# Another order of the seven products of a Strassen-Winograd feed-forward layer, and of the output blocks behind them

## The chip, the core and the metric

One Trainium2 chip, one core of it. The metric is the device time of the whole program in microseconds (us), lower is better. Below, PE is TensorE, DVE is VectorE, ACT is ScalarE, and SP issues the DMAs. "mm" is short for matmul.

## What is computed

A decoder trunk of two layers on 512 positions of width 1024, in float32: layer 0 mixes with a gated MLP and latent attention, layer 1 with gated linear attention. Both end in the same feed-forward half, and the change touches that half alone:

```python
def sqrelu_mlp(x, w1, w2):
    return jnp.square(jax.nn.relu(x @ w1)) @ w2
...
x = layer_norm(ALPHA * x + sqrelu_mlp(x, w_ff1[layer], w_ff2[layer]), ln2_g[layer], ln2_b[layer])
```

`x` is 512 x 1024, `w1` 1024 x 4096, `w2` 4096 x 1024; h = square(relu(x @ w1)) is 512 x 4096.

## The kernel before

**Precision.** Every float32 operand is split into two float32r parts, hi and lo; a product is three matmuls (hi hi, hi lo, lo hi). `split` (L163 to L165) does this for a weight: ACT casts hi (L164), then DVE subtracts lo (L165).

**First product.** `ff` (L283) cuts the 4096 columns of h into 8 groups g of 2 x 256 columns. A group is a 2 x 2 block product: rows of x in two halves, its depth in two halves, and the columns from the left and the right half of w1. Group 0 is done plainly with eight block products. Groups 1 to 7 use seven products of sums (Strassen in Winograd's form): P1, P2, and p3 to p7, listed in `PRODUCTS` (L278). Each is 24 mm of 256 columns (`mul`, L444). Sums of x (s1 to s4) are made once and kept in tiles s2h/s2l, s3h/s3l, s4h/s4l; s1 takes the place of a block of x. Product p3 reads s4, p7 reads s3, p6 reads s2. Sums of weights (t1 to t4) are made on DVE in `sum1` (L369), in place.

**From products to h.** The products go to five PSUM banks a to e (`RELEASED`, L442): P1 and P2 to a, p3 to c, p4 and p7 to d, p5 to e, p6 to b. `product` (L463) issues a product and then whatever has become possible:

```python
            step("V", {"p1s", "p6"}, lambda: nc.vector.tensor_tensor(V, bk("b"), V, ALU.subtract))
            step("X", {"V", "p5"}, lambda: nc.vector.tensor_tensor(X, V, bk("e"), ALU.subtract))
            step("C11", {"P2"}, lambda: relu2(g, 0, 0, bk("a")))
            step("C22", {"X", "p7"}, c22)
            step("C12", {"X", "p3"}, c12)
            step("C21", {"V", "C22", "p4"}, c21)
```

So block C22 of h (second half of the rows, second half of the columns) needs V (L497), X (L498) and r = X - d (L485) on DVE; C12 needs c = X - c (L489); C21 needs d = d - V (L493); C11 comes from its bank directly. Bank d holds p7 until L485 has read it, and only then may p4 be added to it. Each block then goes through `relu2` (L423): ACT relu (L428), ACT square (L429), ACT cast to hh (L430), DVE subtraction hl (L431). The last of these is put in a list `late` and issued by `flush` just before the next product or the next half.

**Second product.** `ff2_half(c, n, t)` (L504) multiplies row block t (128 rows) of h by 256 + 256 rows of w2 for 512 columns n: 12 mm of 512 columns. Blocks t = 0, 1 read C11 for their first 6 mm and C12 for the other 6; t = 2, 3 read C21 and then C22. A chunk c is eight halves, n = 0, 1 by t = 0 to 3; DVE adds each half to the residual XN (L208). Chunk 1 follows group 1 at once, chunk 2 group 2; then come groups 3 and 4 in a row, so that chunks 3, 4, 5 each use blocks that are a group old. Group 7 is followed at once by the close, in which the last two chunks are one sum: for t = 0 first, per n, 6 mm + 6 mm of chunk 6 and then 6 mm of C11 and 6 mm of C12 of group 7 (`close_mm`, L594).

**What sets the order.** PE's order is written out in `slots` (L514 to L522) and kept. DVE's order is that of the program text in this part. ACT's and SP's orders are chosen by a scheduler when the program is built. `wseq` is the order in which weights are loaded and split; `upto` (L543) runs it ahead of PE by up to 6 entries. Split weights of w1 and w2 go through 8 pairs of tiles (whi, wlo). The last four weights of a layer, those of the close for n = 1, go elsewhere (`LAST`, L384, `pair`, L376): the first of them to s4h/s4l, the second to s3h/s3l, the third to s2h/s2l, the fourth to two other tiles. In the profile these four are called ws, and so are three weights of group 0.

Of the kernel before, what the change touches and what calls it, by code (L numbers as in the profile page):

```python
# [22 lines left out]
NT = S // P  # L23
# [80 lines left out]
def trunk(ctx: ExitStack, tc: tile.TileContext, a: dict, out: bass.AP):  # L104
# [179 lines left out]
    def ff(layer, hp, fp, xp, out_proj, prefetch):  # L284

        w1, w2 = a["w_ff1"][layer], a["w_ff2"][layer]
# [68 lines left out]
        def load1(g, n):  # L355

            for m in (n,) if g == 0 else {"B11": ("B11", "B12"), "B21": ("B21",), "t1": ("B22",)}.get(n, ()):
                if g == 0 and m != "B22":
                    raw = wp.tile([P, WG], F32, tag="raw", name="raw", bufs=3)
                elif g == 0 or m in ("B11", "B12"):  # L360
                    raw = xp.tile([P, WG], F32, tag="cr", name="cr", bufs=2)
                else:
                    if g not in kept2:
                        kept2[g] = xp.tile([P, 2, WG], F32, tag="xk", name="cr2")
                    raw = kept2[g][:, m == "B21"]
                raws[g, m] = raw
                nc.sync.dma_start(raw.rearrange("p (k c) -> p k c", k=HK_), w1v(*BLOCK[m], g))

        def sum1(g, n):  # L369

            if n in SUM and (g, n) not in raws:
                x, y = SUM[n]
                raws[g, n] = raws[g, x]
                nc.vector.tensor_tensor(raws[g, n], raws[g, x], raws[g, y], ALU.add)
# [11 lines left out]
        def terms1(g, n):  # L386
            sum1(g, n)
            raw = raws[g, n]
            if (g, n) == (0, "B22"):
                his = [hp.tile([P, HK_, P], F32R, tag="hh", name="wh") for _ in range(2)]  # L390
                los = [hp.tile([P, HK_, P], F32R, tag="hl", name="wl") for _ in range(2)]
                for j in range(2):
                    split(his[j], los[j], raw.rearrange("p (k c) -> p k c", k=HK_)[:, :, tb(j)])
            else:
                hi, lo = pair(EARLY[n] if g == 0 else None)
                split(hi, lo, raw)
                his, los = ([z.rearrange("p (k c) -> p k c", k=HK_)[:, :, tb(j)] for j in range(2)] for z in (hi, lo))
            got_w[g, n] = his, los

        def load2(c, n, half):  # L400
            r = half * 2048 + c * GF
            raw = wp.tile([P, WG], F32, tag="raw", name="raw", bufs=3)
            nc.sync.dma_start(raw.rearrange("p (k c) -> p k c", k=2),
                              w2[r:r + GF, n * 512:(n + 1) * 512].rearrange("(k p) c -> p k c", p=P))
            raws["w2", c, n, half] = raw

        def terms2(c, n, half):
            raw = raws.pop(("w2", c, n, half))
            hi, lo = pair(LAST[(c - NG + 2) * 2 + half] if c >= NG - 2 and n == 1 else None)
            split(hi, lo, raw)  # L410
            v = lambda x: x.rearrange("p (k c) -> p k c", k=2)
            got_w["w2", c, n, half] = v(hi), v(lo)
# [24 lines left out]
        def flush():  # L437
            while late:
                late.pop(0)()
# [23 lines left out]
        def product(g, n):  # L463

            first = (g, RELEASED[n]) not in banks
            if first:
                banks[g, RELEASED[n]] = bank("f1")
            acc = banks[g, RELEASED[n]]
            op, w = PRODUCTS[n]
            mul(acc, op, got_w.pop((g, w)), first)  # L470
            done = state.setdefault(g, set())
            done.add(n)
            V = LG[:, g % 2 * 512:(g % 2 + 1) * 512]
            X = LB[:, g % 2 * 512:(g % 2 + 1) * 512]
            bk = lambda z: banks[g, z]
            hq.setdefault(g, {})

            def step(name, needs, fn):
                if name not in done and needs <= done:
                    done.add(name)  # L480
                    fn()

            def c22():
                r = scratch(g)
                nc.vector.tensor_tensor(r, X, bk("d"), ALU.subtract)  # L485
                relu2(g, 1, 1, r, r)

            def c12():
                nc.vector.tensor_tensor(bk("c"), X, bk("c"), ALU.subtract)  # L489
                relu2(g, 0, 1, bk("c"))  # L490

            def c21():
                nc.vector.tensor_tensor(bk("d"), bk("d"), V, ALU.subtract)  # L493
                relu2(g, 1, 0, bk("d"))

            step("p1s", {"P1"}, lambda: nc.scalar.copy(V, bk("a")))
# [7 lines that stand above are left out]
        def ff2_half(c, n, t):  # L504
            acc = bank("f2")
            i, tc_ = t // 2, slice(t % 2 * P, (t % 2 + 1) * P)
            for k in range(4):
                hh, hl = hq[c][i, k // 2]
                wh, wl = got_w["w2", c, n, k // 2]
                mm3(acc, hh[:, k % 2, tc_], hl[:, k % 2, tc_], wh[:, k % 2], wl[:, k % 2], k == 0, k == 3)  # L510
            add_half(t, n, acc, c == 0, None)


        LATER = ("P1", "p5", "p7", "p6", "p3", "P2", "p4")  # L514
        slots, wseq = [], []

        def put_group(g):
            slots.extend((g, n) for n in LATER)
            wseq.extend((g, n) for n in ("B11", "t1", "t3", "t2", "B22", "B21", "t4"))

        def put_chunk(c):
            slots.extend(("w2", c, n, t) for n in range(2) for t in range(NT))  # L522
            wseq.extend(("w2", c, n, h) for n in range(2) for h in range(2))

        wseq += [(0, n) for n in ("B11", "B21", "B12", "B22")]
        put_chunk(0)

        mid = NG // 2 - 1
        for c in range(1, NG - 2):
            for g in (c,) if c < mid else (c, c + 1) if c == mid else (c + 1,):  # L530
                put_group(g)
            put_chunk(c)
        put_group(NG - 1)
        wseq += [("w2", c, n, h) for n in range(2) for c in (NG - 2, NG - 1) for h in range(2)]
        for i, w in enumerate(wseq):
# [5 lines left out]
        LOADS, TERMS = 6, 6  # L541

        def upto(n, loads=None):  # L543

            while at["load"] < min(len(wseq), n + (LOADS if loads is None else loads)):
                w = wseq[at["load"]]
                at["load"] += 1
                (load2(*w[1:]) if w[0] == "w2" else load1(*w))
            while at["terms"] < min(len(wseq), n):
                w = wseq[at["terms"]]  # L550
                i = at["terms"]
                at["terms"] += 1
                if w[0] != "w2":
                    sum1(*w)
                if i + 1 < at["load"] and wseq[i + 1][1] in SUM and wseq[i + 1] != (w[0], "t1"):
                    sum1(*wseq[i + 1])
                (terms2(*w[1:]) if w[0] == "w2" else terms1(*w))
# [16 lines left out]
        for i, s in enumerate(slots):  # L574
            if s[0] == "w2":
                need = max(place["w2", s[1], s[2], 1], place["w2", s[1], s[2], 0])
                if s[1] == 0:
                    next(sums, None)
                    upto(max(need + 1, 8 + i // 2))
                else:  # L580
                    upto(min(need + 1 + TERMS, need + 1 + 2 * (s[3] + 1)))
                flush()
                ff2_half(s[1], s[2], s[3])
                continue
            upto(place[s[0], PRODUCTS[s[1]][1]] + 1 + min(TERMS, 2 + s[0]))
            flush()
            product(*s)
# [731 lines left out]
    with (tc.tile_pool(name="h0", bufs=8) as hp, tc.tile_pool(name="f0", bufs=2) as fp,  # L1319
          tc.tile_pool(name="x0", bufs=1) as xp, in_order()):  # L1320
        v0 = ff(0, hp, fp, xp, steps, load_v0)
    with tc.tile_pool(name="m1", bufs=1) as mp:
        steps = out_proj_odd(odd_mixer(mp, v0))
    with (tc.tile_pool(name="h1", bufs=8) as hp, tc.tile_pool(name="f1", bufs=2) as fp,
          tc.tile_pool(name="x1", bufs=1) as xp, in_order()):
        ff(1, hp, fp, xp, steps, None)
# [38 lines left out]
```

## Time and profile before

| what | value |
|---|---|
| three runs | 1167.04, 1168.11 (median), 1168.33 us |
| the profiled execution: its own time | 1167.06 us |
| its span, first to last instruction | 1165.4 us |
| PE busy | 1140.8 us, 98% of the span |
| PE weight loads | 994.6 us, 85% |
| DVE busy | 827.6 us, 71% |
| ACT busy | 517.0 us, 44% |
| moved by DMA | 111.68 MB, mean 96 GB/s |

Matmuls are pipelined, so the duration of one (0.28 us for 256 columns, 0.39 us for 512) is longer than the distance to the next. What a matmul costs is read from starts: a run of them without a wait has equal distances, and a wait is a distance that is larger. The profile puts the starts of layer 0's feed-forward half from about 222 to 572 us, and those of layer 1's from about 810 to 1157 us.

### The profile page before, as it was taken

What the parts mean: (1) busy time and instruction counts of PE and PEld (TensorE: products, weight loads), DVE (VectorE), ACT (ScalarE), POOL (GpSimd) and SP (SyncE); (2) the same over time, 40 slices, a digit from 0 to 9 for tenths busy, and PEclk for the clock granted to TensorE, in tenths of its full rate; (3) what the DMA queues carried; (4) which work ended last, traced back from release to release, by engine and by line L of the source; (5) the groups of instructions that cost most, each with busy time, mean ns of one, the idle gap of its engine ahead of it and who ended that gap; (6) DMA issues with size and microseconds to landing.
All of it is one profiled execution on the core that took longest, in us unless ns stands there. A gap on an engine that the chain in (4) does not pass through costs nothing.

```text
span 1165.4 us, 17129 instructions
## 1 busy us (share of the span) xinstructions
PE 1140.8 (98%) x6884; PEld 994.6 (85%) x6884; DVE 827.6 (71%) x1562; ACT 517.0 (44%) x801; POOL 4.5 (0%) x13
## 2 busy tenths in 40 slices
PE   8999999999999999999999999999999999999997
PEld 7988788898889998997888888778997899889986
DVE  6745687786766867658758559898767577676665
ACT  6367462444343634543264433442534436345330
POOL 0000000000000000000000000000000000000000
PEclk9999999999999999999999999999999999999999
DMA  8413143133312342224325312211133224314121
GB/s 269 125 37 109 55 130 107 37 109 109 127 62 84 128 127 84 79 79 135 75 95 145 91 55 73 73 66 62 62 125 116 90 80 142 129 38 127 55 91 55
DMA packets 84207, 111.68 MB, mean 96 GB/s; under 512 B 6080, under 2 KB 53056, under 8 KB 84128
## 3 DMA queue, kind: packets, MB, share of 16 engines
q1 hardware_dynamic: 84128, 110.59, 30.0%
q8 instruction: 54, 0.88, 0.3%
q14 instruction: 25, 0.20, 0.1%
HBM read 108.47 MB, written 2.10 MB: 95 GB/s over the span
## 4 chain that ended last, share of the span: by engine, by line
PE 89%; DVE 6%; ACT 4%; DMA 0%; issue 0%; SPq 0%; DVEq 0%; ACTq 0%
PE f L451 23%; PE f L161 10%; PE f L160 10%; PE f L159 10%; PE vg L159 3%; PE vg L160 3%; PE vg L161 3%; PE op L159 3%; PE op L161 3%; PE op L160 2%; PE sc L843 1%; PE qk L159 1%; PE qk L160 1%; PE qk L161 1%; PE o L865 1%; PE pl L1129 1%
## 5 line engine op out<-in xcount | busy, mean ns | idle before, releaser
L161 PE MATMUL f<-whi,hl 128*128 128x512 f32 x448 | 177.4, 396 | 5.5 <-DVE hl L431 5.5
L159 PE MATMUL f<-whi,hh 128*128 128x512 f32 x448 | 177.2, 396 | 1.0 <-ACT hh L430 1.0
L164 ACT CAST whi<-cr 128x1024 fp32r<-128x1024 f32 x98 | 100.8, 1048 | 174.0 <-PE f L161 81.1
L160 PE MATMUL f<-wlo,hh 128*128 128x512 f32 x448 | 176.8, 395 | 0.0
L164 ACT CAST whi<-raw 128x1024 fp32r<-128x1024 f32 (+3 forms) x117 | 118.4, 1019 | 99.1 <-PE f L451 35.7
L165 DVE TENSOR_TENSOR wlo<-raw,whi 128x1024 fp32r<-128x1024 f32 (+3 forms) x117 | 138.0, 1186 | 26.5 <-ACT whi L164 26.5
L165 DVE TENSOR_TENSOR wlo<-cr,whi 128x1024 fp32r<-128x1024 f32 x98 | 119.3, 1221 | 23.0 <-ACT whi L164 23.0
L451 PE MATMUL f<-XH,wlo 128*128 128x256 f32 x448 | 125.9, 281 | 0.0
L451 PE MATMUL f<-XH,whi 128*128 128x256 f32 x448 | 125.8, 281 | 0.0
L451 PE MATMUL f<-XL,whi 128*128 128x256 f32 x448 | 125.8, 281 | 0.0
L161 PEld LDWEIGHTS f<-whi,hl 128*128 128x128 f32 x448 | 84.3, 188 | 27.7 <-DVE hl L431 8.1
L208 DVE SCALAR_TENSOR_TENSOR XN<-XN,f 128x512 f32<-128x512 f32 (+1 forms) x113 | 74.4, 679 | 42.6 <-PE f L161 42.1
L159 PEld LDWEIGHTS f<-whi,hh 128*128 128x128 f32 x448 | 84.3, 188 | 20.8 <-ACT hh L430 1.8
L160 PEld LDWEIGHTS f<-wlo,hh 128*128 128x128 f32 x448 | 84.3, 188 | 19.3
L451 PE MATMUL f<-sl,whi 128*128 128x256 f32 x336 | 94.6, 281 | 0.0
L451 PE MATMUL f<-sh,wlo 128*128 128x256 f32 x336 | 94.5, 281 | 0.0
L451 PE MATMUL f<-sh,whi 128*128 128x256 f32 x336 | 94.5, 281 | 0.0
L431 DVE TENSOR_TENSOR hl<-r,hh 128x512 fp32r<-128x512 f32 x64 | 44.2, 690 | 60.6 <-ACT hh L430 60.6
L451 PEld LDWEIGHTS f<-XL,whi 128*128 128x128 f32 x448 | 84.4, 188 | 0.5
L451 PEld LDWEIGHTS f<-XH,whi 128*128 128x128 f32 x448 | 84.4, 188 | 0.5
L451 PEld LDWEIGHTS f<-XH,wlo 128*128 128x128 f32 x448 | 84.4, 188 | 0.0
L451 PEld LDWEIGHTS f<-sh,whi 128*128 128x128 f32 x336 | 63.3, 188 | 0.0
(268 smaller groups left out, 2396.8 us busy)
## 6 DMA issues: line engine op xcount, KB each, us to landing
raw<-in_w_ff SPq DMA_DIRECT2D x70, 512.0 KB, 4.1
cr<-in_w_ff SPq DMA_DIRECT2D x58, 512.0 KB, 4.0
raw<-in_w_in_odd SPq DMA_DIRECT2D x24, 512.0 KB, 4.2
XN<-in_x SPq DMA_DIRECT2D x16, 256.0 KB, 3.4
raw<-in_w_in_even SPq DMA_DIRECT2D x8, 512.0 KB, 4.6
raw<-in_w_out_even SPq DMA_DIRECT2D x8, 512.0 KB, 3.8
raw<-in_w_out_odd SPq DMA_DIRECT2D x8, 512.0 KB, 3.6
LB<-in_ln_b SPq DMA_DIRECT2D x4, 512.0 KB, 3.8
```

What stands on the lines that cost most here:

```text
L159: nc.tensor.matmul(acc, lh, rh, start=first, stop=False)
L160: nc.tensor.matmul(acc, lh, rl, start=False, stop=False)
L161: nc.tensor.matmul(acc, ll, rh, start=False, stop=last)
L164: nc.scalar.copy(hi, src)
L165: nc.vector.tensor_tensor(lo, src, hi.bitcast(F32), ALU.subtract)
L208: nc.vector.scalar_tensor_tensor(x, x, ALPHA if first else 1.0, acc, ALU.mult, ALU.add)
L431: late.append(lambda: nc.vector.tensor_tensor(f(hl), r, f(hh).bitcast(F32), ALU.subtract))
L451: nc.tensor.matmul(d, l, r, start=first and j == k == i == 0, stop=j == 1 and k == HK_ - 1 and i == 2, skip_group_check=True)
L843: nc.tensor.matmul(sc[:, :N], qts[t][:B_QK, h, :], KT[:, h, :N], start=True, stop=True)
L865: nc.tensor.matmul(os[t][:, h, :], pT[:, j * P:(j + 1) * P], V[:, j, h, :], start=j == 0, stop=j == t)
L1129: nc.tensor.matmul(pl[:, c * 64:(c + 1) * 64], x[:, tb(c)], x[:, tb(c)].rearrange("p (n two k) -> p n two k", two=2, k=H)[:, :, 1], start= ...
```

## The change

```diff
-        LATER = ("P1", "p5", "p7", "p6", "p3", "P2", "p4")
+        LATER = ("P1", "p5", "p7", "p6", "P2", "p4", "p3")
...
-            wseq.extend((g, n) for n in ("B11", "t1", "t3", "t2", "B22", "B21", "t4"))
+            wseq.extend((g, n) for n in ("B11", "t1", "t3", "t2", "B21", "t4", "B22"))
...
-            slots.extend(("w2", c, n, t) for n in range(2) for t in range(NT))
+
+            slots.extend(("w2", c, n, t, i) for n in range(2) for i, t in enumerate((2, 3, 0, 1) if c else range(NT)))
...
-                    upto(min(need + 1 + TERMS, need + 1 + 2 * (s[3] + 1)))
+                    upto(min(need + 1 + TERMS, need + 1 + 2 * (s[4] + 1)))
```

In groups 1 to 7 product p3 moves from fifth to seventh place, P2 and p4 one place ahead, and the weights follow (B22 is p3's). C12 is now the last block of a group instead of C21. In chunks 1 to 5 the halves run over t = 2, 3, 0, 1, so that a chunk begins with C21 and C22. The close keeps t = 0, 1, 2, 3. No instruction is added or taken away; all line numbers below L521 move by one.

What this does to the order on DVE between group 1 and chunk 1 (r is C22's, hl are the four lo parts of h, wlo are weights of the second product or of the next group). Before:

```order
L485 TENSOR_TENSOR r_3030<-LB_73,f1_2972 128x512
L165 TENSOR_TENSOR wlo_3038<-raw_2830,whi_3037 128x1024
L431 TENSOR_TENSOR hl_3033<-r_3030,hh_3032 128x512
L489 TENSOR_TENSOR f1_3042<-LB_73,f1_3042 128x512
L165 TENSOR_TENSOR wlo_3075<-raw_2865,whi_3074 128x1024
L431 TENSOR_TENSOR hl_3069<-r_3070,hh_3068 128x512
L165 TENSOR_TENSOR wlo_3110<-raw_2926,whi_3109 128x1024
L431 TENSOR_TENSOR hl_3104<-r_3105,hh_3103 128x512
L493 TENSOR_TENSOR f1_2972<-f1_2972,LG_72 128x512
L165 TENSOR_TENSOR wlo_3147<-cr_2928,whi_3146 128x1024
L431 TENSOR_TENSOR hl_3140<-r_3141,hh_3139 128x512
```

Now:

```order
L485 TENSOR_TENSOR r_3030<-LB_73,f1_2972 128x512
L165 TENSOR_TENSOR wlo_3038<-raw_2830,whi_3037 128x1024
L431 TENSOR_TENSOR hl_3033<-r_3030,hh_3032 128x512
L165 TENSOR_TENSOR wlo_3073<-raw_2865,whi_3072 128x1024
L431 TENSOR_TENSOR hl_3067<-r_3068,hh_3066 128x512
L493 TENSOR_TENSOR f1_2972<-f1_2972,LG_72 128x512
L165 TENSOR_TENSOR wlo_3110<-raw_2926,whi_3109 128x1024
L431 TENSOR_TENSOR hl_3103<-r_3104,hh_3102 128x512
L489 TENSOR_TENSOR f1_3114<-LB_73,f1_3114 128x512
L165 TENSOR_TENSOR wlo_3147<-cr_2928,whi_3146 128x1024
L431 TENSOR_TENSOR hl_3141<-r_3142,hh_3140 128x512
```

The lo parts were those of C22, C12, C11, C21 in this order, and are those of C22, C11, C21, C12 now; L489 (for C12) and L493 (for C21) have changed places. On ACT the steps of C11 were paired with those of C12 (relu, relu, square, square, cast, cast) in groups 1 and 2; in every group they are now paired in the same way with those of C22.

On ACT at the seam of groups 3 and 4, the last block of group 3 (C21 before, C12 now) behind the copy L496 of group 4's first product; whi from raw are the weights of chunk 3. Before:

```order
L496 COPY LG_72<-f1_3937 128x512
L428 ACTIVATE r_3919<-f1_3739 128x512
L429 ACTIVATE r_3919<-r_3919 128x512
L164 CAST whi_3932<-cr_3547 128x1024
L430 CAST hh_3917<-r_3919 128x512
L164 CAST whi_3963<-raw_3764 128x1024
L164 CAST whi_3992<-raw_3806 128x1024
L164 CAST whi_4021<-raw_3846 128x1024
```

Now:

```order
L496 COPY LG_72<-f1_3937 128x512
L164 CAST whi_3963<-raw_3764 128x1024
L428 ACTIVATE r_3920<-f1_3892 128x512
L164 CAST whi_3992<-raw_3806 128x1024
L429 ACTIVATE r_3920<-r_3920 128x512
L164 CAST whi_4022<-raw_3844 128x1024
L430 CAST hh_3918<-r_3920 128x512
```

Three casts of weights that stood behind the last block now stand between its steps.

On ACT and DVE in group 7 and up to the close of layer 0 (ws from raw_5040 or raw_5041 is the first of the four last weights, the one that is written to s4h/s4l). DVE before:

```order
L485 TENSOR_TENSOR r_5200<-LB_73,f1_5144 128x512
L165 TENSOR_TENSOR wlo_5208<-raw_5020,whi_5207 128x1024
L431 TENSOR_TENSOR hl_5203<-r_5200,hh_5202 128x512
L489 TENSOR_TENSOR f1_5212<-LB_73,f1_5212 128x512
L165 TENSOR_TENSOR ws_5245<-raw_5040,ws_5244 128x1024
L431 TENSOR_TENSOR hl_5239<-r_5240,hh_5238 128x512
```

DVE now:

```order
L431 TENSOR_TENSOR hl_5203<-r_5200,hh_5202 128x512
L165 TENSOR_TENSOR ws_5243<-raw_5041,ws_5242 128x1024
L431 TENSOR_TENSOR hl_5237<-r_5238,hh_5236 128x512
L493 TENSOR_TENSOR f1_5144<-f1_5144,LG_72 128x512
L165 TENSOR_TENSOR ws_5279<-raw_5043,ws_5278 128x1024
L431 TENSOR_TENSOR hl_5273<-r_5274,hh_5272 128x512
L489 TENSOR_TENSOR f1_5283<-LB_73,f1_5283 128x512
L165 TENSOR_TENSOR ws_5316<-raw_5107,ws_5315 128x1024
L165 TENSOR_TENSOR ws_5320<-raw_5138,ws_5319 128x1024
L431 TENSOR_TENSOR hl_5310<-r_5311,hh_5309 128x512
```

ACT before:

```order
L164 CAST ws_5279<-raw_5042 128x1024
L428 ACTIVATE r_5200<-r_5200 128x512
L164 CAST ws_5244<-raw_5040 128x1024
L429 ACTIVATE r_5200<-r_5200 128x512
L430 CAST hh_5202<-r_5200 128x512
L428 ACTIVATE r_5275<-f1_5081 128x512
```

ACT now:

```order
L430 CAST hh_5202<-r_5200 128x512
L430 CAST hh_5236<-r_5238 128x512
L164 CAST ws_5315<-raw_5107 128x1024
L164 CAST ws_5242<-raw_5041 128x1024
L428 ACTIVATE r_5274<-f1_5144 128x512
L429 ACTIVATE r_5274<-r_5274 128x512
L430 CAST hh_5272<-r_5274 128x512
L164 CAST ws_5319<-raw_5138 128x1024
L428 ACTIVATE r_5311<-f1_5283 128x512
L429 ACTIVATE r_5311<-r_5311 128x512
L430 CAST hh_5309<-r_5311 128x512
```

The first of the four last weights stood behind L489, that is, behind the whole of p3, on DVE; now it stands ahead of the lo part of C11, of L493 and of L489, and on ACT its cast stands ahead of the relu of C21. Layer 1 has the same orders at all three places.

## Rows read from the trace of the kernel before

**Rows 1.** The page: the chain that ended last, by engine.

```profile
PE 89%; DVE 6%; ACT 4%; DMA 0%; issue 0%; SPq 0%; DVEq 0%; ACTq 0%
```

**Rows 2.** Waits of PE, the longest group: us in total, times, longest.

```profile
PE f L161 <- DVE hl L431: 5.5, 6, 1.2
```

**Rows 3.** Timeline of PE, group 1 to chunk 1: start, duration, instruction, idle before.

```profile
289.46 0.28 PE L451 MATMUL f<-XH,wlo 128*128 128x256 f32 x1
289.94 0.50 PE L159 MATMUL f<-whi,hh 128*128 128x512 f32 x1 [0.20 <-ACT hh L430]
290.28 0.40 PE L160 MATMUL f<-wlo,hh 128*128 128x512 f32 x1
291.89 0.50 PE L161 MATMUL f<-whi,hl 128*128 128x512 f32 x1 [1.22 <-DVE hl L431]
```

**Rows 4.** Timeline of DVE, the same stretch.

```profile
281.25 0.69 DVE L497 TENSOR_TENSOR LG<-f,LG 128x512 f32<-128x512 f32 x1 [4.92 <-PE f L451]
...
282.70 0.69 DVE L485 TENSOR_TENSOR r<-LB,f 128x512 f32<-128x512 f32 x1
...
285.40 0.69 DVE L431 TENSOR_TENSOR hl<-r,hh 128x512 fp32r<-128x512 f32 x1 [0.88 <-ACT hh L430]
286.01 0.69 DVE L489 TENSOR_TENSOR f<-LB,f 128x512 f32<-128x512 f32 x1
...
290.01 1.22 DVE L165 TENSOR_TENSOR wlo<-raw,whi 128x1024 fp32r<-128x1024 f32 x1
291.15 0.69 DVE L431 TENSOR_TENSOR hl<-r,hh 128x512 fp32r<-128x512 f32 x1
291.75 0.69 DVE L493 TENSOR_TENSOR f<-f,LG 128x512 f32<-128x512 f32 x1
...
294.42 0.69 DVE L431 TENSOR_TENSOR hl<-r,hh 128x512 fp32r<-128x512 f32 x1 [0.85 <-ACT hh L430]
```

**Rows 5.** Timeline of ACT, the same stretch.

```profile
286.74 1.09 ACT L428 ACTIVATE r<-f 128x512 f32<-128x512 f32 x2 [1.36 <-DVE f L489]
...
288.75 1.14 ACT L430 CAST hh<-r 128x512 fp32r<-128x512 f32 x2
```

**Rows 6.** Timelines of DVE and ACT, the seam of groups 3 and 4.

```profile
381.59 0.69 DVE L493 TENSOR_TENSOR f<-f,LG 128x512 f32<-128x512 f32 x1
...
386.29 3.49 DVE L165 TENSOR_TENSOR wlo<-raw,whi 128x1024 fp32r<-128x1024 f32 x3
389.70 0.68 DVE L497 TENSOR_TENSOR LG<-f,LG 128x512 f32<-128x512 f32 x1
...
384.94 2.95 ACT L164 CAST whi<-raw 128x1024 fp32r<-128x1024 f32 x3
```

**Rows 7.** Timeline of PE, last products of group 7 and start of the close.

```profile
518.85 0.28 PE L451 MATMUL f<-XH,whi 128*128 128x256 f32 x1
...
524.52 0.40 PE L159 MATMUL f<-whi,hh 128*128 128x512 f32 x1
...
527.54 0.40 PE L160 MATMUL f<-wlo,hh 128*128 128x512 f32 x1
528.27 0.50 PE L161 MATMUL f<-whi,hl 128*128 128x512 f32 x1 [0.32 <-DVE hl L431]
```

**Rows 8.** Timeline of ACT there: the cast into s4h.

```profile
519.05 1.05 ACT L164 CAST ws<-raw 128x1024 fp32r<-128x1024 f32 x1
```

**Rows 9.** The page: DMA issues of these weights, KB each, us to landing.

```profile
raw<-in_w_ff SPq DMA_DIRECT2D x70, 512.0 KB, 4.1
```

**Rows 10.** A stretch at the end: PE, PEld, DVE, ACT, POOL busy, granted clock, DMA.

```profile
1161.00:1162.00 1.00, 0.00 (x0) 0.00 (x0) 1.00 (x2) 0.00 (x0) 0.00 (x0) 0.77 0.00 0
```

**Rows 11.** Timelines of PE: its first instructions, and its last.

```profile
1.15 2.93 PE L885 MATMUL warm<-idle 128*128 128x128 f32 x12 [1.15 <-DVE idle L880]
...
5.54 0.72 PE L885 MATMUL warm<-idle 128*128 128x128 f32 x5
...
1157.13 0.28 PE L161 MATMUL f<-ws,hl 128*128 128x256 f32 x1
```

## The prediction

> **What bounds the kernel now.** I read the chain that ended last first: PE holds 89% of it [rows 1], so only what lets PE wait, or takes work from it, can change the time. The change takes no work from PE: the same matmuls run in another order. Next come PE's waits. One group of them belongs to this part: six waits for the lo part of a block of h, 5.5 us in all [rows 2]. The timeline of PE shows where [rows 3]; to read it, take the distances without a wait from [rows 7]: 48 mm of the products from 518.85 to 524.52, 0.118 us each, so a product of 24 takes 2.84; 13 mm of the second product from 524.52 to 527.54, 0.232 each.
>
> At group 1's end the last mm starts at 289.46 [rows 3], so chunk 1 is due at 289.58. It starts at 289.94, 0.36 late, waiting for hh of C11. The next mm follows 0.34 later, not 0.23: a restart costs 0.11. The third starts 1.61 after that, 1.38 late, waiting for hl of C11; with another 0.1 for the restart the place costs 1.95 us. Chunk 2 repeats the pattern, and layer 1 repeats both: four places, 7.8 us. At the close the 15th mm starts 0.73 after the 14th [rows 7], 0.50 late, 0.6 with its restart; two layers, 1.2 us. These 9.0 us are all that the change can win. 0.2% is 2.3 us, about what a measurement of this kernel can tell from no change.
>
> Why is C11 late? DVE's timeline [rows 4] shows its steps in file: L489 waits behind an hl, the hl of C11 behind a weight's split (290.01). From the start of L493 to the start of its hl takes 2.67 us (291.75 to 294.42), which is relu, square and cast on ACT. Back to back, DVE's starts are 0.60 apart for a block and 1.14 for a weight (290.01, 291.15, 291.75). When ACT pairs two blocks its starts are 0.50 apart: four steps from 286.74 to 288.75 [rows 5].
>
> **The change, place by place.** No instruction is added, so the sum is of waits.
>
> *Chunks 1 and 2.* p6 is seen by DVE at 281.25 [rows 4]; now P2 is done at 284.09, p4 at 286.93, p3 at 289.77. L485 ends at 283.39. ACT takes the relu of C22, then that of C11, which waits for P2 until 284.09; 0.50 a step puts the cast of C22 at 285.6, ending at 286.25 (0.62 long). hl of C22 starts at 286.3 (before: 285.40), a weight's split at 286.9, hl of C11 at 288.0, L493 at 288.6 though p4 was done at 286.93, and 2.67 later, at 291.3, hh of C21 is done and its hl starts. C21 is what chunk 1 now begins with: 1.7 late on 289.58. Its third mm is due at 291.9 and hl ends at 292.0, 0.1 more; two restarts, 0.2. That is 2.1 us, against 1.95: the wait is as long as before, for another block. C12, last now, is safe: hl by 295.7 at the latest, first read 30 mm (7.0 us) after 291.3. Bounds: one ACT step, 0.5, either way for each place. I take +0.15 for each of four: **+0.6 us** (-2.0 to +2.6).
>
> *Groups 3 and 4.* Chunk 3's blocks are a group old, so no wait for h is expected there. But p4 adds to bank d, which L485 must have read, and p4 is now second behind p6 instead of third: L485 ends 2.14 after L497 starts (281.25 to 283.39, [rows 4]) and p4 starts 2.84 after PE is done with p6. That leaves 0.5 us where L497 starts on time, and in group 4 it does not. Before, DVE was busy up to L497 there (three splits from 386.29, L497 at 389.70 without idle, [rows 6]), so it was just in time. Now the last block of group 3 has three casts of weights between its steps on ACT, 2.95 us [rows 6]. L489 stands where L493 was, at about 382.0 by the same walk (before 381.59); it would have its hl 2.67 later, at 384.7, and has it at 387.4. The three splits take 3.4 and a block 0.6, so L497 starts at 391.4 and L485 ends at 393.5. PE is due at p4 at 392.3 (L497 could have started by 389.6, PE's last mm of p6 is about 0.2 before that, and P2 takes 2.84). The stall is 1.2 us per layer. Bounds: none, if DVE is as early as before, and 2.5. **+2.5 us** in two layers (0 to +5). In the other groups DVE is idle ahead of L497, as in group 1 (4.92 us, [rows 4]), and the 0.5 us hold.
>
> *The close.* This is the large term. The first of the layer's last four weights is written to s4h/s4l, the tiles that p3 reads. Before, p3 was third from the end, and the cast started at 519.05 [rows 8], 0.2 after PE had gone on to P2 at 518.85 [rows 7]. Now p3 ends where the close begins, 524.52, so the cast runs from 524.72 to 525.77. On DVE its lo part stands ahead of hl of C11, L493 and L489, and DVE keeps its file: lo part at 525.8, hl of C11 at 526.9 (done 527.6, read at 527.77: just in time), L493 at 527.5 although p4 ended at 521.7, hl of C21 at 530.2, L489 at 530.8, done at 531.5. ACT then has the fourth weight ahead of the relu of C12: its buffer is free at 527.0, it lands 4.1 later [rows 9], and its cast (starts 0.95 apart from the next, as in the 2.95 for three of [rows 6]) lets the relu start at 532.05; relu, square and cast end at 534.0, hl at 534.7. PE needs C12 for the 19th mm, due at 528.70: 5.3 late, then 0.1 for hl and 0.2 for restarts, 5.6 us, against 0.6 before. **+10.0 us** in two layers (+8.6 with a landing after 3.5 us, +10.8 with all waits for the landing 0.4 longer).
>
> [...]
>
> *What lies beside.* The loads of the next group's second pair wait for one split more (1.14 us); they have a chunk of 96 x 0.232 = 22 us. The layer norm's LG is loaded ahead of LB now, both over 5 us before the first norm, which PE's delay puts off as well. Halves in another order add to other rows of XN, at the same price. All three: nothing.
>
> The sum is 0.6 + 2.5 + 10.0 = 13.1 us: 1180.2 on the profiled execution's 1167.06. The runs' median is 1.05 above it, so the forecast is **1181.2 us**, 1.1% slower.
>
> **Rivals.** *Faster:* C21 is ready when p3 ends, the four places are empty, and the cast into s4 passes unseen. That needs L493 to start by 286.9 in place of 288.6, so DVE must have done the split and both hl 1.7 us earlier. It would give 1168.1 - 7.8 - 1.2 = 1159.1. Against it: r cannot end before 283.39, and what follows is a file. 3%. [...] 38%. *The close hides the cast:* something I took as in file isn't, and only chunks 1, 2 and group 4 count: 1168.1 + 3.1 - 1.2 = 1170.0. 5%. *No effect:* one wait for another everywhere, 1168.1. 2%.
>
> **How the numbers follow.** My forecast has 52%. Its own bounds, -2.0 + 0 + 8.6 to 2.6 + 5 + 10.8, give 1174.7 to 1186.5, ends that need all terms at their bounds together; I take 1176.5 to 1185.5, which holds both cases of the clock too and leaves out the three others and the outermost of these two. Faster by over 0.2%: 3%. Within: the hidden cast and no effect, 7%. Slower: 90%.
>
> **What would show it.** Right: a wait of PE of about 5 us for hh of C12, 19 mm into each close; the cast of ws into s4 at the end of p3 with DVE idle until then; a wait of some 1 us at p4 of group 4; four waits of about 2 us at chunks 1 and 2, now for C21. [...] Wrong: a close without a wait over 1 us, or chunks 1 and 2 starting on time.

## The result, and the profile after

| what | before | after |
|---|---|---|
| median of the runs compared (lowest to highest) | 1167.57 us (1166.96 to 1168.33, 4 runs) | 1184.35 us (1183.30 to 1185.54, 4 runs) |
| ratio, with 95% interval | | 1.0144 [1.0131, 1.0156] |
| the profiled execution, its span | 1167.06 us, 1165.4 us | 1185.15 us, 1183.4 us |
| mean granted clock over the span | 0.998 | 0.991 |

The changed kernel is slower by 1.4%. The chain that ended last, by engine, answers to [rows 1]: PE's share fell from 89% to 86%, and DVE's and ACT's did not take all of it.

```profile
PE 86%; DVE 6%; ACT 5%; DMA 1%; issue 1%; SPq 0%; DVEq 0%; ACTq 0%
```

PE's waits (us in total, times, longest). The wait for hl of [rows 2], 5.5 us, is gone. Two others stand in its place, for hh of a block of h (six times) and for r in front of p4 (twice):

```profile
PE f L159 <- ACT hh L430: 15.5, 6, 4.6
PE f L451 <- DVE r L485: 2.0, 2, 1.0
```

**Chunk 1 of layer 0**, timeline of PE (start, duration, instruction, idle before), beside [rows 3]:

```profile
289.67 0.28 PE L451 MATMUL f<-sh,wlo 128*128 128x256 f32 x1
291.52 0.50 PE L159 MATMUL f<-whi,hh 128*128 128x512 f32 x1 [1.56 <-ACT hh L430]
291.85 0.39 PE L160 MATMUL f<-wlo,hh 128*128 128x512 f32 x1
292.24 0.50 PE L161 MATMUL f<-whi,hl 128*128 128x512 f32 x1
292.58 0.39 PE L159 MATMUL f<-whi,hh 128*128 128x512 f32 x1
```

Four distances, 2.91 us from the first row to the last, where 0.12 and three times 0.232 would be 0.81: 2.10 us are lost, all but 0.37 of it in front of the first mm. Before, it was 1.95, most of it in front of the third. DVE in the same stretch, beside [rows 4]:

```profile
281.47 0.69 DVE L497 TENSOR_TENSOR LG<-f,LG 128x512 f32<-128x512 f32 x1 [4.60 <-PE f L451]
...
288.23 0.69 DVE L431 TENSOR_TENSOR hl<-r,hh 128x512 fp32r<-128x512 f32 x1
288.83 0.69 DVE L493 TENSOR_TENSOR f<-f,LG 128x512 f32<-128x512 f32 x1
...
291.50 0.69 DVE L431 TENSOR_TENSOR hl<-r,hh 128x512 fp32r<-128x512 f32 x1 [0.85 <-ACT hh L430]
```

L493 begins the way to C21 right behind the hl of C11, and 2.67 us later C21's hl starts, as before. C21, with which chunk 1 now begins, is ready no earlier than C11 was before.

**Seam of groups 3 and 4**, DVE, then PE, beside [rows 6]:

```profile
388.24 3.49 DVE L165 TENSOR_TENSOR wlo<-raw,whi 128x1024 fp32r<-128x1024 f32 x3
391.64 0.68 DVE L497 TENSOR_TENSOR LG<-f,LG 128x512 f32<-128x512 f32 x1
...
393.08 0.69 DVE L485 TENSOR_TENSOR r<-LB,f 128x512 f32<-128x512 f32 x1
```

```profile
392.54 0.28 PE L451 MATMUL f<-XH,wlo 128*128 128x256 f32 x1
393.82 0.39 PE L451 MATMUL f<-XH,whi 128*128 128x256 f32 x1 [1.00 <-DVE r L485]
394.05 0.28 PE L451 MATMUL f<-XL,whi 128*128 128x256 f32 x1
```

DVE comes from three splits without a pause, so L485 ends at 393.77, and p4, due at 392.66, starts at 393.82. With the next mm's 0.11 the place costs 1.27 us. Layer 1 has the same wait.

**The close of layer 0**, ACT, DVE and PE, beside [rows 7, 8]:

```profile
526.38 1.05 ACT L164 CAST ws<-raw 128x1024 fp32r<-128x1024 f32 x1 [0.56 <-PE f L451]
529.93 0.60 ACT L428 ACTIVATE r<-f 128x512 f32<-128x512 f32 x1 [2.50 <-DVE f L493]
...
532.20 1.05 ACT L164 CAST ws<-raw 128x1024 fp32r<-128x1024 f32 x1 [0.36 <-DMA raw<-in_w_ff]
533.20 0.60 ACT L428 ACTIVATE r<-f 128x512 f32<-128x512 f32 x1
...
534.49 0.62 ACT L430 CAST hh<-r 128x512 fp32r<-128x512 f32 x1
```

```profile
527.46 1.22 DVE L165 TENSOR_TENSOR ws<-raw,ws 128x1024 fp32r<-128x1024 f32 x1 [3.90 <-ACT ws L164]
528.60 0.68 DVE L431 TENSOR_TENSOR hl<-r,hh 128x512 fp32r<-128x512 f32 x1
529.20 0.69 DVE L493 TENSOR_TENSOR f<-f,LG 128x512 f32<-128x512 f32 x1
...
532.48 0.69 DVE L489 TENSOR_TENSOR f<-LB,f 128x512 f32<-128x512 f32 x1
```

```profile
530.14 0.40 PE L161 MATMUL f<-whi,hl 128*128 128x512 f32 x1
535.16 0.79 PE L159 MATMUL f<-whi,hh 128*128 128x512 f32 x1 [4.62 <-ACT hh L430]
535.75 0.63 PE L160 MATMUL f<-wlo,hh 128*128 128x512 f32 x1
536.18 0.70 PE L161 MATMUL f<-whi,hl 128*128 128x512 f32 x1
536.68 0.63 PE L159 MATMUL f<-whi,hh 128*128 128x512 f32 x1
...
540.50 0.39 PE L159 MATMUL f<-ws,hh 128*128 128x512 f32 x1
540.73 0.40 PE L160 MATMUL f<-ws,hh 128*128 128x512 f32 x1
```

DVE idles 3.90 us until the cast of the weight that goes to s4h, which itself waited for PE to be done with p3 (the releaser of 526.38). Only then come hl of C11, L493 and L489, and the 19th mm waits for the hh of C12: it starts 4.79 late. Then the mm follow each other 0.43 apart, not 0.232, up to 540.50. From 530.14 to 540.73 there are 14 distances, 10.59 us; at 0.232 they would be 3.25. The close loses 7.34 us.

The 0.43 is the clock. Stretches of the same execution (length, busy us of PE, PEld, DVE, ACT, POOL with counts, granted clock, DMA share, GB/s):

```profile
533.50:540.50 7.00, 5.34 (x12) 3.98 (x13) 4.80 (x6) 3.31 (x5) 0.00 (x0) 0.51 0.93 336
884.00:888.60 4.60, 3.04 (x20) 2.32 (x19) 3.75 (x7) 2.94 (x5) 0.00 (x0) 1.00 0.55 172
888.60:892.10 3.50, 3.50 (x10) 2.72 (x9) 1.75 (x3) 1.80 (x3) 0.00 (x0) 0.51 0.20 78
1130.90:1137.90 7.00, 5.46 (x13) 4.08 (x14) 3.85 (x6) 2.71 (x4) 0.00 (x0) 0.51 0.23 85
```

The granted clock stood at 0.50 for 6.8 us in each close, and for 3.4 us in chunk 1 of layer 1, behind a wait of only 1.56 (the 0.51 are means with the edges of a stretch). Timeline of PE there:

```profile
888.30 0.39 PE L159 MATMUL f<-whi,hh 128*128 128x512 f32 x1
...
892.17 0.39 PE L160 MATMUL f<-wlo,hh 128*128 128x512 f32 x1
```

Ten distances from 888.30 to 892.17 took 3.87 in place of 2.32, a loss of 1.55.

**The sum of the profiled execution**: chunks 1 and 2, 4 x (2.10 - 1.95) = 0.6; p4 of group 4, 2 x 1.27 = 2.5; the closes, 2 x (7.34 - 0.6) = 13.5; the clock in layer 1's chunk, 1.55. Together 18.15, and 1185.15 - 1167.06 = 18.09. No term of any size is missing; that the two agree to 0.06 is closer than the readings are, since this execution also comes 0.21 later to the feed-forward half of layer 0 (223.00 against 222.79), where nothing was changed.

### The profile page after: what moved, and what is told of

The parts are those of the page before. It is cut to its first block, busy times and chain, and to the rows that moved or that the text cites. A ratio compares the mean times of both kernels' runs of the same rounds, so it can differ in the third digit from the quotient of the medians.

```text
span 1183.4 us, 17118 instructions
## 1 busy us (share of the span) xinstructions
PE 1147.7 (97%) x6884; PEld 999.3 (84%) x6884; DVE 827.4 (70%) x1562; ACT 517.3 (44%) x801; POOL 4.9 (0%) x13
## 4 chain that ended last, share of the span: by engine, by line
PE 86%; DVE 6%; ACT 5%; DMA 1%; issue 1%; SPq 0%; DVEq 0%; ACTq 0%
PE f L451 21%; PE f L159 10%; PE f L161 10%; PE f L160 10%; PE vg L159 3%; PE vg L160 3%; PE vg L161 3%; PE op L159 2%; PE op L161 2%; PE op L160 2%; PE sc L844 1%; PE qk L159 1%; DVE wlo L165 1%; PE qk L160 1%; PE qk L161 1%; PE o L866 1%
## 5 line engine op out<-in xcount | busy, mean ns | idle before, releaser
L451 PEld LDWEIGHTS f<-sl,whi 128*128 128x128 f32 x336 | 63.3, 188 | 0.0
```

The source lines that it names most:

```text
L451: nc.tensor.matmul(d, l, r, start=first and j == k == i == 0, stop=j == 1 and k == HK_ - 1 and i == 2, skip_group_check=True)
```

## Experiments

Theory: three places cost as predicted, and in the closes the clock costs some 2 us beside the wait. Rivals are named with each run. Times before are medians of the runs on the same chip.

**Which tile the close's first weight goes to.** The changed kernel, with s4h/s4l given to the last of the four weights:

```diff
-        LAST = [("s4h", "s4l"), ("s3h", "s3l"), ("s2h", "s2l"), ("cr", "cr")]
+        LAST = [("s3h", "s3l"), ("s2h", "s2l"), ("cr", "cr"), ("s4h", "s4l")]
```

> The changed kernel, but the four last weights of a layer go to other tiles: the first to s3, the second to s2, the third to the two loose ones, the fourth to s4. Theory: the close waits because the cast into s4 must see the end of p3 and DVE's file stands behind it; with s4 taken last, hh of C12 is done about 1.4 us late in place of 4.8, the clock does not fall there, and the time is about 1173 (1184.35 less twice 5.6). Rival: C12 is late simply because it is the last block now; then the close still waits over 4 us and the time stays within 2 us of 1184.

Measured: 1171.45 us (before 1166.83), ratio 1.0040 [1.0025, 1.0055]. Some 12 us of the loss (1.0144 - 1.0040 of 1167) come back with one line that moves no product. In the close, PE:

```profile
531.11 0.50 PE L159 MATMUL f<-whi,hh 128*128 128x512 f32 x1 [0.68 <-ACT hh L430]
...
532.01 0.50 PE L161 MATMUL f<-whi,hl 128*128 128x512 f32 x1 [0.17 <-DVE hl L431]
```

The wait is 0.68 us instead of 4.62, and the granted clock is 1.00 throughout the close. So the cost was the cast into s4h with what stands behind it in DVE's file, not the late p3 as such. That C12 comes last still costs about 1.4 us per close (0.85, 0.33 and two restarts).

**Groups 7 and 4 apart.** The changed kernel with the old order of products and weights in group 7 alone, and in group 4 alone:

```diff
-            slots.extend((g, n) for n in LATER)
+            slots.extend((g, n) for n in (("P1", "p5", "p7", "p6", "p3", "P2", "p4") if g == NG - 1 else LATER))
...
```

> The changed kernel with group 7 alone in the old order of products and weights. Theory: this takes away the whole term of the close with the clock's fall behind it; the close waits 0.5 us per layer as before the change, and the time is about 1171 (1184.35 less twice 6.7). What is left above the kernel before is then chunks 1 and 2 and the seam, about 3 us. Rival (the loss is spread over all groups): above 1177.

> The changed kernel with group 4 alone in the old order. Theory: the wait of 1.16 us at p4 of group 4 is there because p4 follows p6 with one product between and L485 has to have read bank d; with two products between the wait goes, L497 is still late by about 2 us, and the time is about 1182 (less 2.5). Rival: DVE's lateness at the seam costs PE anyway, at the next product or at a weight; then a wait of about 1 us stands elsewhere in group 4 or chunk 3 and the time does not move.

Group 7 (in the diff; for group 4 the condition is g == mid + 1): 1171.73 us, ratio 1.0041 [1.0026, 1.0056]; the close waits 0.49 as before the change, the other waits stay. Its profiled execution had one low stretch, at chunk 1 of layer 1 again:

```profile
881.60:885.10 3.50, 3.50 (x10) 2.72 (x9) 1.91 (x3) 1.51 (x3) 0.00 (x0) 0.52 0.14 52
```

Group 4: 1179.91 us, ratio 1.0112 [1.0095, 1.0129]. No wait of PE for r is left, in either layer, and L485 ends 1.5 us earlier. By the ratios that is 3.7 us less than the changed kernel, where the two waits were 2.5; its profiled execution has only 3.4 us of low clock in layer 1's close (0.51 from 1128.60 to 1132.10) and none at the chunks. The waits are shown to be gone; that the other 1.2 us are the clock's is argued from that one execution, and the two intervals leave room for it to be chance. One part of the expectation missed: L497 was to stay about 2 us late, and it starts on time (390.14, 0.19 behind PE). With this edit ACT again does its three casts of weights behind the last block of group 3 (385.11 to 388.06) instead of between its steps, and the block's hl starts at 385.86 instead of 387.63. So two things changed at once, the casts and the distance from p6 to p4. Which of them would be enough alone was not run; the times say that the casts would, since L485 then ends at 392.28 and p4 as second behind p6 was due at 392.66.

**The clock apart from the wait.** The changed kernel with spare matmuls (pads) of an identity into an unused bank, ahead of the 19th mm of the close; PE waits there anyway. First 36, then 18:

```diff
+                if (t, n, k) == (0, 0, 6):
+                    pad = bank("warm", "tp")
+                    for _ in range(18):
+                        nc.tensor.matmul(pad[:, :P], ident, ident, start=True, stop=True)
```

> The changed kernel with 36 spare matmuls of 128 columns on PE ahead of the 19th of each close (about 4.0 us of PE, into a bank nobody reads). They lie in the wait of 4.8 us, so the wait for hh of C12 shrinks to under 1 us and the block comes no sooner. Theory: the fall of the granted clock costs about 2 us per layer by itself; with PE kept at work it does not fall at the close and the time is about 1180. Rival: the slow matmuls behind the wait are part of the same lateness, and the time stays at 1184 or goes up.

36 were too many: 1187.65 us, ratio 1.0169 [1.0154, 1.0185]. Each shows as two records, so the pads took 8 us:

```profile
529.87 8.20 PE L601 MATMUL warm<-ident 128*128 128x128 f32 x72
```

They outlast the wait, so the time says little. In the profiled execution (1184.54, mean clock 0.998) the mm behind them ran at 0.23 and no stretch was low; the other three runs, at 1187.57 to 1187.91, have a mean clock of 0.995, and where it fell in them no profile shows.

> The changed kernel, with 18 spare f32 matmuls of 128 columns ahead of the close's 19th matmul, half of the 36 of the run before, which took 7.96 us in all and so 0.221 us each: here 4.0 us, less than the 5.2 us between the 18th matmul and the 19th. Theory (the wait itself is 4.8 us late per close with its restarts about 5.2, and the clock's fall costs the other 2 us of the 7.35): the 19th matmul starts where it does in the changed kernel, within 0.5 us, no granted clock of 0.5 in the closes, the matmuls after it at 0.232 us, time 1184.35 - 2 x 2 = about 1180.4. Rival (the slow matmuls behind the wait are slow for another reason, such as reads of h beside the engines that write it): they stay at 0.43 us and the time at 1184.

18: 1181.56 us (before 1166.90), ratio 1.0123 [1.0109, 1.0137]. Timeline of PE:

```profile
533.19 0.40 PE L161 MATMUL f<-whi,hl 128*128 128x512 f32 x1
533.42 4.18 PE L601 MATMUL warm<-ident 128*128 128x128 f32 x36
538.22 0.50 PE L159 MATMUL f<-whi,hh 128*128 128x512 f32 x1 [0.62 <-ACT hh L430]
538.55 0.39 PE L160 MATMUL f<-wlo,hh 128*128 128x512 f32 x1
539.14 0.50 PE L161 MATMUL f<-whi,hl 128*128 128x512 f32 x1 [0.20 <-DVE hl L431]
539.48 0.39 PE L159 MATMUL f<-whi,hh 128*128 128x512 f32 x1
```

The 19th mm is due at 533.42 and starts 4.80 late, as in the changed kernel; the pads move nothing. Behind it the distances are those of the full clock (granted 1.00 from 535.00 to 540.00). From 533.19 to 539.48, four distances, 5.36 us are lost: this is the wait with its restarts, and 7.34 - 5.36 = 1.98 us is what the clock costs in this close. Layer 1 agrees: from the first mm of its close to its last the changed kernel takes 51.78 us, this one 49.75. The rival, that reads of h beside the engines that write it slow these mm, falls: the same engines write at the same time here. The median came 1.2 above the 1180.4 expected, and by the ratios only some 2.4 us of the 4.0 are won (1.0144 - 1.0123 of 1167). The closes of the profiled execution do win their 4.0. It loses elsewhere: it comes 1.5 us later than the changed kernel's to the feed-forward half of layer 0 (224.47 against 223.00), where the pads change nothing, and it has a low stretch of 3.4 us at chunk 1 of layer 0 (granted clock 0.56 from 293.50 to 297.40), as the changed kernel's has one in layer 1. What the other three runs lost, no profile shows.

**The order of the halves.** The changed kernel with t = 0 to 3 in chunks 1 to 5, so that a chunk begins with C11 and then reads C12, which now comes last:

```diff
-            slots.extend(("w2", c, n, t, i) for n in range(2) for i, t in enumerate((2, 3, 0, 1) if c else range(NT)))
+            slots.extend(("w2", c, n, t, i) for n in range(2) for i, t in enumerate(range(NT)))
```

> The changed kernel with the halves of chunks 1 to 5 in the old order t = 0, 1, 2, 3; products as changed. Theory: a chunk may then start on time, since C11 is ready, but reads C12, the last block, at its 7th matmul, due 1.4 us after p3's end, while hh of C12 needs about 5 us from there: a wait of about 3.6 us and 0.3 at four places in place of 2.1, so about 1191, more where the clock falls behind it. Rival: it does not matter with which block a chunk begins, since DVE's file sets the end; then the time stays at 1184.

Measured: 1196.85 us (before 1168.18), ratio 1.0249 [1.0235, 1.0263]. The wait moves to the 7th mm of the chunk, PE:

```profile
290.78 0.39 PE L161 MATMUL f<-whi,hl 128*128 128x512 f32 x1
294.63 0.80 PE L159 MATMUL f<-whi,hh 128*128 128x512 f32 x1 [3.46 <-ACT hh L430]
295.22 0.63 PE L160 MATMUL f<-wlo,hh 128*128 128x512 f32 x1
```

```profile
294.00:297.50 3.50, 2.87 (x7) 2.25 (x8) 0.69 (x1) 0.58 (x1) 0.00 (x0) 0.51 0.00 0
```

All four such waits of 3.46 us in the profiled execution, whose mean clock is 0.988, are followed by 3.4 us of low clock. Four falls at some 1.5 us each are what lies between the measured time and about 1191. So the halves of the change belong to its order of products: given that order, they save some 12 us (1.0249 - 1.0144 of 1167).

**What a smaller swap does.** The kernel before, with only P2 ahead of p3 (C12 stays ahead of C21, halves as they were):

```diff
-        LATER = ("P1", "p5", "p7", "p6", "p3", "P2", "p4")
+        LATER = ("P1", "p5", "p7", "p6", "P2", "p3", "p4")
...
-            wseq.extend((g, n) for n in ("B11", "t1", "t3", "t2", "B22", "B21", "t4"))
+            wseq.extend((g, n) for n in ("B11", "t1", "t3", "t2", "B21", "B22", "t4"))
```

> The kernel before with one step only: P2 moved ahead of p3 (P1, p5, p7, p6, P2, p3, p4), B21 ahead of B22, halves in the old order. Theory: C11 and C12 then go through DVE and ACT ahead of C21, C11 is ready when a chunk begins, hh of C12 comes about 0.3 us late for the 7th matmul, p4 stays third behind p6, and at the close the cast into s4 ends before DVE would need it: four places at 0.65 in place of 1.95 and nothing at the close, 1167.6 less 6.4, about 1161. Rival: every order gives one wait of about 2 us for another; then 1167 to 1168.

Measured: 1160.78 us (before 1168.18), ratio 0.9937 [0.9924, 0.9951]. Chunks 1 and 2 start on time; all that is left is a wait at the 7th mm, four times:

```profile
292.95 0.50 PE L159 MATMUL f<-whi,hh 128*128 128x512 f32 x1 [0.18 <-ACT hh L430]
```

Here C11 is paired with C22 and the block that follows, C12, is first read by the 7th mm. The close has no wait. Both together with the other tiles in `LAST`:

> The single step (P2 ahead of p3 in the kernel before) with s4 taken by the fourth of the last weights instead of the first. If the cast into s4 still costs something at the close there, this is faster than the single step alone; the theory says it costs nothing there, so the two agree within 1 us, about 1161.

1160.66 us, ratio 0.9938 [0.9925, 0.9950]: the same. With p3 sixth instead of seventh, the cast into s4h is early enough.

**Chunks a group behind.** The kernel before, with groups 1 and 2 in a row instead of 3 and 4; then this with the swap:

```diff
-        mid = NG // 2 - 1
+        mid = 1
```

> The kernel before with groups 1 and 2 in a row instead of groups 3 and 4, so that every chunk uses blocks that are a group old. Theory: the four waits at chunks 1 and 2 go (7.8 us) and only the close's are left: about 1160. Rival: the waits hide a lack of weights; groups 1 and 2 in a row need 14 products' weights from DVE with the shorter lead of the first groups, and PE waits for a wlo or whi instead: 1165 or more.

> The kernel before with two edits that each came out faster alone: P2 ahead of p3 (with B21 ahead of B22), and groups 1 and 2 in a row so that every chunk's blocks are a group old. Theory (both take away the waits at chunks 1 and 2, and the swap takes away those of the close as well): 1158.72 less the two close waits of 0.6 us, about 1157.5. Rival (groups 1 and 2 in a row bring a wait of their own that the old order hides): over 1160, with a wait of PE in group 2.

1158.72 us (before 1168.18), ratio 0.9922 [0.9908, 0.9935], and 1157.52 us (before 1166.90), ratio 0.9917 [0.9903, 0.9930]. In the first, only the close's 0.49 is left; in the second PE's longest group of waits is one outside the feed-forward half:

```profile
PE pt L856 <- ACT qt L826: 1.4, 3, 0.7
```

The second's span is 1155.9 against 1157.0, the 1.1 us of two close waits; by the ratios, taken on two chips, the two versions can't be told apart. By [rows 3, 7] the first was to win the 7.8 us of chunks 1 and 2, and the second the 9.0 us of these and the close. The spans of the profiled executions, 1165.4 before, say 8.4 and 9.5. Rivals of both expectations (lack of weights, a new wait in group 2) did not show.

## Why the prediction was right, and where its point was low

The sign and the range held (1176.5 to 1185.5); the point, 1181.2, is 3.15 us under the median. Step by step:

- **Chunks 1 and 2**, +0.6. The prediction's walk gave C21's hl at 291.3, 2.1 us for the place. Measured: 291.50 (L497 itself 0.22 later than the walk assumed), 2.10. Right, and for the stated reason: one block's wait replaced another's. (Its lower bound, -2.0, doesn't follow from its own 0.5 us either way on +0.15 for each place, which gives -1.4.)
- **p4 of group 4**, +2.5. L497 at 391.4, stall 1.2; measured 391.64 and 1.27. The old order in group 4 takes the wait away, and the casts on ACT that the prediction named go back behind the block with it. Right.
- **The close**, +10.0. The mechanism is shown by the change of tiles alone. Its working is in times of before; group 7 ends 1.68 later now (the 18th mm at 530.14 puts the first at 526.20, against 524.52). With that added: cast 526.40 (measured 526.38), L493 529.2 (529.20), L489 532.5 (532.48). The fourth weight's cast was put at 532.8 and came at 532.20, since its load landed sooner: the landing taken was [rows 9]'s 4.1; this load was issued at 528.71 and landed some 3.5 later, and the page of after has 3.7 as the median:

```profile
raw<-in_w_ff SPq DMA_DIRECT2D x70, 512.0 KB, 3.7
```

So C12's relu waited for L489's end, 533.17, as much as for that weight, and the place cost 5.36 (from the run with 18 pads) instead of 5.6. In two layers the term is 9.5 instead of 10.0. The prediction's own figure for a landing of 3.5 was +8.6; its times, with the relu held by L489's end, give +8.9.
- **The clock** is the step that failed, as a choice. The forecast of 52% had it stay up at the close; 38% stood for a fall there. It fell in both layers: +1.98 each by the pads, and the median is 1184.35. The range was meant to hold both cases, but no row read ahead of the result showed what a fall inside the kernel costs; the 1.98 and the 1.55 are the first figures for it. I had weighed the one fall in the trace of before as too little to forecast from. That fall lies in the stretch of [rows 10], between these two:

```profile
1158.00:1161.00 3.00, 0.00 (x0) 0.00 (x0) 2.83 (x9) 0.29 (x1) 0.00 (x0) 1.00 0.00 0
1162.00:1165.40 3.40, 0.00 (x0) 0.00 (x0) 0.17 (x1) 0.00 (x0) 0.00 (x0) 0.50 0.41 154
```

From 1.00 to 0.50 with a mean of 0.77 puts it at 1161.54, 4.4 us after the start of PE's last work (1157.13, [rows 11]). The wait that I forecast, 5.3 late and so 5.5 from start to start, was longer than that by a quarter. In the close of layer 0 the clock fell sooner, 3.5 us after the start of PE's last work (530.14; the granted clock of 533.00 to 534.00 is 0.82), in a wait of 5.0. In the three profiled executions that have the wait of 4.6 us without pads in both layers, it falls six times of six (mean clocks of the three: 0.991, 0.993, 0.988).
- **What none of my cases had** is a fall of the clock at a chunk. The runs of the changed kernel lie in two pairs, 1183.30 and 1183.54 with a mean clock of 0.993, 1185.15 and 1185.54 with 0.991. The profiled one is of the upper pair and has the extra 3.4 us; 3.4 x 0.5 / 1183 is 0.0014 of the mean clock. That the other upper run has it too is argued from the clock, not seen.

The terms of the profiled execution without the chunk's fall are 0.6 + 2.5 + 9.5 + 4.0 = 16.6; on 1168.1 that is 1184.7, on the 1167.57 of this comparison 1184.2, against the 1184.35 measured.

## What to carry to other kernels

When products change places, look at which tiles are overwritten behind the last reader, not only at who waits for whose result: here a line that gives the recycled tile to the last weight instead of the first was worth some 12 us of 16.8. Before reordering to start with "the block that is ready longest", walk the in-order engine that makes the blocks: ready is when its file lets it be, and moving another block forward moved the wait to that block. In these runs the granted clock fell to 0.5 behind a wait of PE 4 of 4 times after 3.46 us, 6 of 6 after 4.6 and 3 of 24 after 1.56; the place then cost the wait and the slow mm behind it (1.98 us more in a close, 1.55 in a chunk), so price both.

## What was not expected of the hardware

- The clock fell behind a short wait too. In six profiled executions (the changed kernel, the two with `LAST` and group 7, group 4, and the two with pads) chunks 1 and 2 wait 1.56 us, 24 times in all, and three of the 24 are followed by 3.4 us of low clock (0.51 from 888.60 to 892.10 in the changed kernel, 0.52 from 881.60 to 885.10 with group 7 in the old order, 0.56 from 293.50 to 297.40 with 18 pads), at a cost of 1.55 us in the one worked out above. All three are at a chunk 1, layer 1's twice and layer 0's once, and none at a chunk 2; why these three stays open. The run of the smaller swap has one more outside the feed-forward half: 3.4 us from 24.84 on (granted clock 0.51 from 24.80 to 28.30), behind a wait of 2.0 us that ended at 23.98; the mean clock of that execution is 0.996, of the other four 0.998 or 0.999. Before the change, the one profiled execution shows none behind its four waits of 1.2 us (mean clock 0.998). But the 25 runs of that kernel beside the experiments lie in two groups: 15 from 1166.2 to 1167.6, and 10 from 1168.1 to 1169.0, with a mean clock of 0.997 in place of 0.998 or 0.999. One low stretch of 3.4 us would explain both the time (1.55) and the clock (3.4 x 0.5 / 1167 = 0.0015), and the two kernels without waits at chunks have no such second group in nine runs; no profile shows it.
- A low stretch lasted 3.4 or 6.8 us behind the same wait of 4.6 us: 6.8 in both closes of the changed kernel, 6.8 and 3.4 in the two of the run with group 4 in the old order, and likewise in the run with the halves in the old order. In the closes its first part overlaps the wait (in layer 0 of the changed kernel the clock is at 0.50 by 533.70, and the 19th mm starts at 535.16), so 6.8 us of low clock cost 1.98 and not 3.4.
- An f32 matmul of 128 columns shows as two records, and 36 of them took 8.0 us: 0.22 us each, about as long as a float32r matmul of 512 columns (0.232).
